# One written order for TensorE from the key tiles on, new places for its small steps, and eight block stores on ScalarE's queue

## The chip, the cores and the metric

The kernel runs on one core of one Trainium2 chip. Five engines work side by side, each through its own instructions in order: TensorE (PE in the profile, its weight loads PEld), VectorE (DVE), ScalarE (ACT), GpSimd (POOL) and SyncE (SP), which issues most transfers. The metric is device time in microseconds (us) of the whole program, the median of three runs.

## The reference

One layer of a hybrid decoder, for a sequence of 256 positions and a width of 2048, all in float32:

```
h    = rms_norm(x, attn_norm_g)
proj = h @ w_in                          # 2048 -> 4448 columns
r, k, v, w, a, g = split(token_shift(proj[: shifted part]))
c_q, c_kv, k_pe  = split(proj[rest])
y_rwkv = rwkv7_mixer(r, k, v, w, a, g)   # 16 heads of 64: a recurrence over positions,
                                         # then group norm, a bonus term and a gate
y_mla  = mla_mixer(c_q, c_kv, k_pe)      # 8 heads: up-projections, rotary keys, causal softmax
x = x + concat(y_rwkv, y_mla) @ w_out
h = rms_norm(x, ffn_norm_g)
x = x + (silu(causal_conv3(h @ w_gate)) * (h @ w_up)) @ w_down     # 5632 wide
out = rms_norm(x, final_norm_g)
```

The recurrence per head and position is state = state * w + (state a) b + v k, y = state r. The kernel computes it in four chunks of 64 positions: inside a chunk as products of matrices (Gram matrices, a triangular solve), and from chunk to chunk through the state.

## The kernel before, in words

**Big products.** Every weight comes from memory in pieces of 128 x 1024 float32 (`piece`, line 125). ScalarE casts a piece to a rounded part `hi` (line 133), VectorE makes the rest `lo` (line 134), and TensorE multiplies hi by both parts of the activations and lo by the high part. Three buffers each hold raw pieces, `hi` and `lo`. A tile of the input projection is 128 columns for all 256 positions: two pieces of 24 matmuls each, `in_tile` (line 194) or, written as a generator, `part_c` (line 789). `yield`s divide it into steps of eight matmuls, three steps a piece, six a tile. Tile 0 is the two low-rank inputs, 1 to 8 the keys, 9 to 16 the r's, 17 to 24 the values, 25 and 26 gate and rotary key, 27 to 34 the latents of attention.

**Small products between them.** Each key tile is normalized, shifted (`shifted`), multiplied into its block, squared, and its squares summed by `key_ss` (line 475). `decay` (line 411) forms four pairs of head groups' decays from the low-rank tile: eight records of `lw` and eight of `la` on TensorE (line 420), one on rows 0 to 63 and the other on rows 64 to 127, and a chain on ScalarE and VectorE. `key_norms` and `key_norms_p` turn the sums of squares into norms (`pmt`, line 500). After an r tile come its `bonus` sums (line 526), and after every second one `gram` (line 529): for a pair of head groups the products of two chunks at a time, on two row halves `h` (line 542), masked by VectorE into `G1` (line 547), and three transposes of the block (line 562). After the second and the fourth pair the corner blocks of G1 go to memory, 16 stores each, on SP's queue (line 555). `solve_load` reads them back, and `solve` (line 586) is a chain of 62 VectorE operations with two round trips to memory behind it, which leave the inverse in `TT` and `T11`. `values` transposes the value tiles (line 632).

**The recurrence.** `corner_r`, `corner_t` (R, T) complete the inverses with 32 x 32 products (lines 648, 661). Then for each chunk and each half of the heads: `rows` and `rows_state` (w, x), `solved` (i), `update` of the state (u), `out_state` and `out_local` (s, o), each 16 records of 64-wide products (line 686) with copies on VectorE or ScalarE between dependent ones.

**PSUM.** Eight banks: three `mm` for big products, three `ch` and two `at` for the rest. The bonus sums hold a `ch` bank through all r tiles. The key sums hold an `at` bank until the norms are formed.

**What sets the order.** The tile framework places every instruction of an engine by a simulated timeline, except where an order is fixed by hand. Up to the value tiles it places TensorE's work itself; the small steps are put on a list (`pend`) and issued behind the next tile. From the latents on, TensorE's order is fixed (`manual_schedule`, line 1137): `STREAM` is the list of big products, cut into steps, and `PLAN` the list of small steps; a number in PLAN is how many steps of the stream go before the next small step. Other engines' orders stay with the framework. The letters are in `small` (line 1120): for instance `w00`, `R0`, `S1` (scores of head 1), `P` (transposed weights of attention), `A` (attention's product), `N`, `G`, `Y` (group norm, gate and transposes), `X` (transposes of the sum x). In STREAM `l` is a latent tile, `q`, `Q`, `K`, `v` up-projections, `W` the output projection, `F` the first half of the feed-forward part.

## Time and profile before

| | before |
|---|---|
| median of three runs | 1170.52 us (1168.86 to 1172.1) |
| profiled execution: time | 1171.28 us |
| profiled execution: span | 1169.3 us, granted TensorE clock 0.995 on average |
| TensorE busy | 1151.5 us, 98% |
| VectorE busy | 807.0 us, 69% |
| ScalarE busy | 610.0 us, 52% |
| read from memory | 210.85 MB, 183 GB/s over the span |

The span runs from the first to the last instruction. Matmuls are pipelined and their ends are modelled, so "busy" is not "at full rate": in a timeline the distance from one start to the next says more. A matmul of 64-wide or larger float32 operands leaves two records. The granted clock is the share of full speed that the chip allowed TensorE in a stretch.

### The profile page before, as it was taken

To read this page: it belongs to the slowest core of one execution; us is meant where nothing else is said; L and a number is where in the kernel's file an instruction comes from. 1 tells how busy PE (TensorE), PEld (TensorE's weight loads), DVE (VectorE), ACT (ScalarE), POOL (GpSimd) and SP (SyncE) were. 2 spreads that over 40 slices of the span, in tenths; PEclk is the share of its full clock that TensorE was granted. 3 is DMA by queue.
4 is the path that set the end of the run, shared out by engine and by line. 5 is a ranking of instruction groups with operands and counts; after the bars stand their busy time and mean duration, and the time that the engine had idled before them with its cause. 6 is when DMAs were issued, how large, how long until landed. Compare 5 with 4: busy or idle time off the path is not lost.

```text
span 1169.3 us, 19472 instructions
## 1 busy us (share of the span) xinstructions
PE 1151.5 (98%) x7669; PEld 1018.2 (87%) x7669; DVE 807.0 (69%) x1333; ACT 610.0 (52%) x912; POOL 18.5 (2%) x45
## 2 busy tenths in 40 slices
PE   9999999999999999999999999999999999999996
PEld 9899999999878888888888888888888888888885
DVE  6897669746997577777767774544677777775653
ACT  6884346445653465555555553333455555554441
POOL 1200000000000000000000000000000000000000
PEclk9999999999999999999999999999999999999999
DMA  9645456715635555555555655665555565576672
GB/s 329 198 142 166 136 166 199 216 46 163 194 126 178 193 175 175 197 184 196 194 191 192 197 189 190 197 190 192 195 198 190 189 198 185 194 234 199 209 216 79
DMA packets 71227, 216.24 MB, mean 185 GB/s; under 512 B 17648, under 2 KB 18032, under 8 KB 71136
## 3 DMA queue, kind: packets, MB, share of 16 engines
q1 hardware_dynamic: 70208, 212.89, 56.2%
q10 hardware_dynamic: 576, 1.39, 0.4%
q8 instruction: 60, 0.98, 0.4%
q0 software_dynamic: 352, 0.72, 0.3%
q14 instruction: 31, 0.25, 0.1%
HBM read 210.85 MB, written 3.41 MB: 183 GB/s over the span
## 4 chain that ended last, share of the span: by engine, by line
PE 88%; DMA 4%; DVE 3%; ACT 2%; issue 1%; SPq 1%; ACTq 0%; DVEq 0%
PE mm L1080 27%; PE mm L1091 14%; PE mm L808 8%; PE mm L189 7%; PE mm L187 7%; PE mm L188 7%; PE mm L164 5%; PE mm L793 3%; PE mm L167 3%; PE mm L867 2%; DVE lo L134 1%; PE px L686 1%; PE pg L542 1%; DMA raw<-in_win 1%; PE py L686 1%
## 5 line engine op out<-in xcount | busy, mean ns | idle before, releaser
L134 DVE TENSOR_TENSOR lo<-raw,hi 128x1024 fp32r<-128x1024 f32 x376 | 459.8, 1223 | 269.2 <-ACT hi L133 198.9
L133 ACT CAST hi<-raw 128x1024 fp32r<-128x1024 f32 x376 | 395.7, 1053 | 422.5 <-PE mm L1080 126.1
L1080 PE MATMUL mm<-z,hi 128*128 128x512 f32 x1408 | 351.7, 392 | 0.8 <-DVE z L1032 0.8
L1080 PEld LDWEIGHTS mm<-z,hi 128*128 128x128 f32 x1408 | 251.5, 188 | 44.3 <-DVE z L1032 1.2
L1091 PEld LDWEIGHTS mm<-z,lo 128*128 128x128 f32 x1408 | 186.4, 188 | 14.9
L1091 PE MATMUL mm<-z,lo 128*128 128x256 f32 x1408 | 189.1, 276 | 0.0
L189 PE MATMUL mm<-hi,hl 128*128 128x512 f32 x336 | 130.7, 389 | 0.0
L188 PE MATMUL mm<-lo,hh 128*128 128x512 f32 x336 | 130.7, 389 | 0.0
L187 PE MATMUL mm<-hi,hh 128*128 128x512 f32 x336 | 119.7, 389 | 0.0
L164 PE MATMUL mm<-x,hi 128*128 128x256 f32 x768 | 103.0, 282 | 0.2 <-ACT hi L133 0.2
L164 PEld LDWEIGHTS mm<-x,hi 128*128 128x128 f32 x768 | 93.8, 188 | 2.0 <-ACT hi L133 0.4
L189 PEld LDWEIGHTS mm<-hi,hl 128*128 128x128 f32 x336 | 63.1, 188 | 13.2
L188 PEld LDWEIGHTS mm<-lo,hh 128*128 128x128 f32 x336 | 63.1, 188 | 13.1
L187 PEld LDWEIGHTS mm<-hi,hh 128*128 128x128 f32 x336 | 63.0, 188 | 12.9
L167 PE MATMUL mm<-x,lo 128*128 128x256 f32 x384 | 55.3, 281 | 0.0
L808 PE MATMUL mm<-hi,yhi 128*128 128x512 f32 x128 | 50.7, 396 | 0.0
L808 PE MATMUL mm<-lo,yhi 128*128 128x512 f32 x128 | 50.5, 395 | 0.0
L808 PE MATMUL mm<-hi,ylo 128*128 128x512 f32 x128 | 50.3, 393 | 0.0
L167 PEld LDWEIGHTS mm<-x,lo 128*128 128x128 f32 x384 | 48.8, 188 | 1.1 <-issue 1.0
L793 PE MATMUL mm<-x,hi 128*128 128x256 f32 x256 | 34.6, 286 | 0.0
L793 PEld LDWEIGHTS mm<-x,hi 128*128 128x128 f32 x256 | 31.6, 192 | 0.7
L808 PEld LDWEIGHTS mm<-hi,ylo 128*128 128x128 f32 x128 | 24.1, 188 | 5.3 <-DVE ylo L965 0.4
(294 smaller groups left out, 1120.6 us busy)
## 6 DMA issues: line engine op xcount, KB each, us to landing
raw<-in_wgu SPq DMA_DIRECT2D x176, 512.0 KB, 3.3
raw<-in_wdn SPq DMA_DIRECT2D x88, 512.0 KB, 4.2
raw<-in_win SPq DMA_DIRECT2D x70, 512.0 KB, 3.9
raw<-in_wout SPq DMA_DIRECT2D x32, 512.0 KB, 3.3
raw<-in_wuq SPq DMA_DIRECT2D x6, 512.0 KB, 4.4
xraw<-in_xT SPq DMA_DIRECT2D x4, 512.0 KB, 6.1
xt<-in_x SPq DMA_DIRECT2D x4, 512.0 KB, 7.5
raw<-in_wuv SPq DMA_DIRECT2D x4, 512.0 KB, 4.8
```

Of the source, the lines that this page charges most:

```text
L133: S.copy(hi, raw)
L134: last_lo[0] = V.tensor_tensor(lo, raw, hi.bitcast(F32), ALU.subtract).ins
L164: PE.matmul(acc[:, :T], hi[:, j * P:(j + 1) * P], act(kt0 + j)[:, s, :], start=first and j == 0 and s == 0, stop=False)
L167: i = PE.matmul(acc[:, :T], lo[:, j * P:(j + 1) * P], act(kt0 + j)[:, 0, :], start=False, stop=last and j == n - 1)
L187: PE.matmul(accs[tb], ah, wh, start=first and j == 0, stop=False)
L188: PE.matmul(accs[tb], ah, wl, start=False, stop=False)
L189: i = PE.matmul(accs[tb], al, wh, start=False, stop=last and j == n - 1)
L686: PE.matmul(dst[HS[h], a_ * 64:(a_ + 1) * 64], lhsT, rhs, start=begin and a_ == 0, stop=True, skip_group_check=True)
L793: PE.matmul(acc[:, :T], w[:, j * P:(j + 1) * P], act(j)[:, s, :], start=first and m == 0, stop=last and m == len(ops) - 1)
L808: PE.matmul(accs[tb], act, w, start=first and j == 0 and act is ah and w is wh, stop=last and j == 1 and act is al)
L1080: PE.matmul(accs[i], pcs[p][0][:, j * P:(j + 1) * P], z_hl(h * 8 + j), start=i not in seen, stop=False, skip_group_check=True)
L1091: PE.matmul(accs[i][:, :T], lo[:, j * P:(j + 1) * P], z_hl(h * 8 + j)[:, 0, :], start=False, stop=last and j == 7, skip_group_check=True)
```

## The change

TensorE's order is now fixed from the fourth key tile on, by the same STREAM and PLAN, and both lists are new. `pend` and `flush` are gone; key, r and value tiles become steps of the stream (`t4` to `t24`), and what was on the list becomes small steps with letters of their own. Two pieces of work are done in another way: the second half of a Gram product takes its two banks from `at` instead of `ch`, and of the last 16 corner stores the eight of the second row half are issued by ScalarE's queue.

```
+    def front_tile(i):
+        acc = mm()
+        for h in range(2):
+            yield from part_c(acc, piece(a["win"][i, h]), lambda k: x_hl(h * 8 + k), 8, h == 0, h == 1)
+            if h == 0:
+                yield
+        if i < 9:
+            key_done(i - 1, acc)
+        elif i < 17:
+            r_done(i - 9, acc)
+        else:
+            vt[i - 17] = shifted(acc, i)
+        yield
...
     def decay(pp):
-        with tc.high_priority(), tc.manual_schedule(engines={mybir.EngineType.PE}):
-            for g in range(2):
+        for g in range(2):
...
-        def gram(p=p, pp=pp):
+    def gram(pp, w):
...
-            for w in range(2):
-                pg = [ch("pg") for _ in range(2)]
+        pg = [(at if w else ch)("pg") for _ in range(2)]
...
-                            nc.sync.dma_start(dLv[b, c, :, h, hf * 4:hf * 4 + 4, :],
+                        (nc.scalar if h and hf else nc.sync).dma_start(
+                            dLv[b, c, :, h, hf * 4:hf * 4 + 4, :],
...
+    def turn_b(pp):
...
+        for cs in ((0, 1), (2,)):
+            pt = ch("pt")
...
     def solve():
+        for c in range(4):
+            nc.gpsimd.memset(UV[c][64:128], 0.0)
...
     small = {
-        "o": out_local, "r": latent_root, "b": spread, "c": swap, ...
+        "o": out_local, "r": latent_root, "f": spread, "c": swap, ...
+        "n": norm2, "D": decay, "E": key_done, "k": key_ss, "t": turn_b, "m": key_norms, "p": key_norms_p, "b": bonus,
+        "a": gram, "B": bonus_rows, "L": solve_load, "Z": solve, "V": values,
     }
     STREAM = """
-    l00 l01 l02 l03 l10 l11 l12 l13 q1 q0 v0 K0 Q0 K1 Q1 v1 K2 Q2 K3 Q3 W100 W110 W120 W130 W001 W021
-    W011 W031 F
+    t4 t5 t6 t7 t8 t9 t10 t11 t12 t14 t13 t15 t16 t18 t17 t20 t19 t21 t23 t22 t24 l00 l01 l02 l03 l10
+    l11 l12 l13 q0 q1 v0 K0 Q0 Q1 K2 K1 Q2 v1 K3 Q3 W100 W110 W120 W130 W001 W021 W011 W031 F
     PLAN = """
-    12 w00 18 r0 4 R0 R1 T0 w01 1 i00 i01 w11 u00 u01 w10 o01 T1 x11 x10 o00 s10 i10 i11 s11 u10 w20 u11
-    w21 o10 o11 1 x20 x21 1 s21 2 i20 w30 i21 1 s20 u20 u21 w31 1 o21 1 o20 x31 x30 s31 1 g 1 i31 i30 1
-    s30 1 o30 6 r1 o31 7 b1 c 4 e 7 S0 S1 5 S3 S2 1 P0 1 N0 4 P1 h0 2 P3 h1 A0 1 A1 1 S4 1 P2 1 S5 A2 1 A3 3
-    S6 2 P4 3 P5 A4 A5 S7 2 P6 1 P7 A6 A7 9 N1 1 G10 5 G00 2 G01 5 Y01 11 Y10 1 Y00 4 G11 2 Y11 26 X00
-    11 X10 X21 4 X01 4 X11 2 X20 2 X30 X31 9 n
+    2 D0 1 E0 E1 2 D1 E2 4 k1 k0 2 D2 5 k2 1 D3 5 k4 1 k3 7 k5 7 t0 1 k6 6 t1 k7 1 m 1 p a00 1 t2 a01 b1
+    7 b0 3 b2 2 t3 b3 2 a10 a11 5 b5 4 a20 a21 5 b4 3 b6 2 a30 2 b7 B a31 4 L 1 Z 19 V0 10 V1 2 w00 12
+    V2 12 V3 14 R1 2 R0 1 w01 1 T0 1 i00 i01 w11 u00 u01 w10 o01 x11 o00 x10 i11 s10 i10 s11 w20 u10 w21
+    u11 o10 1 x21 T1 x20 r0 1 o11 1 s21 s20 i20 i21 3 g o21 w30 3 u20 w31 h1 u21 o20 x30 x31 i30 s31 s30
+    i31 6 o30 3 r1 4 o31 2 f1 1 c 1 e 5 S1 3 h0 1 S0 8 S3 2 S2 2 P0 P1 N0 3 A1 S4 1 A0 P3 1 P2 2 S5 A3
+    A2 2 P4 S6 5 P5 S7 A4 P6 A5 2 A6 N1 P7 1 A7 3 G10 17 G00 2 G01 9 G11 1 Y10 2 Y11 1 Y01 2 Y00 32 X01
+    9 X21 3 X10 X00 3 X11 5 X31 2 X20 X30 5 n
```

`b` is the bonus sums now, and the old `b` is `f`. `h0` and `h1` split the gate's weights; `g` loads group norm's weights. The text below calls a place in the new order by the sum of the numbers ahead of it in PLAN: R1 stands at step 156, and the 21 tiles of the stream's first part fill steps 1 to 126.

## The prediction

> **What bounds the kernel now.** I read the page's first part, then TensorE's waits, then TensorE's timeline with its starts, since a start-to-start distance shows lost time that a busy share hides.

> ```profile
> PE 1151.5 (98%) x7669; PEld 1018.2 (87%) x7669; DVE 807.0 (69%) x1333; ACT 610.0 (52%) x912; POOL 18.5 (2%) x45
> ```

> TensorE is busy 98% of a span of 1169.3 us. The change removes no matmul, so it can only gain where TensorE's instructions stand further apart than they need to. Everything it moves lies between some 43 us (the fourth key tile) and 420 us (the second norm); behind that the two kernels issue the same work. TensorE's waits in the front part (37 to 205 us) are few:

> ```profile
> PE lw L420 <- ACT early L396: 0.8, 1, 0.8
> PE la L420 <- DVE hb L177: 0.4, 1, 0.4
> PE pv L632 <- DVE sh L386: 0.2, 1, 0.2
> PE ssP L475 <- ACT ksq L471: 0.2, 1, 0.2
> ...
> PE pT L661 <- ACT RT L652: 0.4, 1, 0.4
> PE pT L661 <- DMA TT<-dT: 0.3, 1, 0.3
> ```

> The last two are of the recurrence. These six sum to 2.3 us: shown waits alone would not repay a new order. The rest sits in instructions that are busy but slow, and the timeline finds it.

> **Part 1, the gram products: -5.1 us.** The columns are start, time, instruction, and how many records.

> ```profile
> 98.14 1.98 PE L164 MATMUL mm<-x,hi 128*128 128x256 f32 x16
> 99.95 1.08 PE L167 MATMUL mm<-x,lo 128*128 128x256 f32 x8
> ...
> 101.30 1.16 PE L542 MATMUL pg<-AR,BK 64*128 64x128 f32 x16
> 102.39 2.15 PE L164 MATMUL mm<-x,hi 128*128 128x256 f32 x16
> ...
> 105.65 1.16 PE L542 MATMUL pg<-AR,BK 64*128 64x128 f32 x8
> 106.73 0.38 PE L164 MATMUL mm<-x,hi 128*128 128x256 f32 x1
> 107.05 1.16 PE L542 MATMUL pg<-AR,BK 64*128 64x128 f32 x8
> 108.13 1.74 PE L164 MATMUL mm<-x,hi 128*128 128x256 f32 x13
> ...
> 155.29 1.16 PE L542 MATMUL pg<-AR,BK 64*128 64x128 f32 x8
> ```

> Sixteen records on the two halves of the rows, issued in turns, take 102.39 - 101.30 = 1.09 us. The other half-gram of the same pair is split by the free buffers: eight records of one row half, one big matmul, eight of the other. It runs from 105.65 to 108.13; less 0.12 us for the big matmul between, that is 2.36 us for the same work. Before, both halves of a gram draw on the three `ch` buffers, of which the bonus sums hold one; the change takes the second half's two tiles from the two `at` buffers and issues the halves in turns. So the second half should also take 1.09 us: 1.27 us saved, four times (this first one; the last is the split one that ends the list) = 5.1 us. At nothing in return: the two `at` buffers are free once the key sums have been read, and the first gram stands behind the key norms in the new order.

> **Part 2, the decay products: -0.9 us.**

> ```profile
> 46.35 0.48 PE L420 MATMUL lw<-early,lora 64*128 64x256 f32 x1 [0.80 <-ACT early L396]
> ...
> 47.42 0.74 PE L167 MATMUL mm<-x,lo 128*128 128x256 f32 x4
> ...
> 50.78 0.70 PE L420 MATMUL la<-early,lora 64*128 64x256 f32 x2 [0.36 <-DVE hb L177]
> 51.41 0.38 PE L167 MATMUL mm<-x,lo 128*128 128x256 f32 x1
> 51.72 0.48 PE L420 MATMUL lw<-early,lora 64*128 64x256 f32 x1
> ...
> 52.78 0.62 PE L167 MATMUL mm<-x,lo 128*128 128x256 f32 x3
> ```

> The first decay is whole, 1.07 us. The second is torn: 50.78 to 52.78 less one big matmul is 1.9 us, so 0.8 us too long. Of the other two one is torn as well, by a shorter piece; 0.6 us is my estimate from the second's 0.8. The new order issues each whole: -1.4. Against that D0 now stands two steps into the fourth key tile. A step is eight matmuls: 1.81 us for sixteen (98.14 to 99.95) make 0.91 us. It comes some 0.45 us earlier than before while its tanh comes no earlier: +0.5.

> **Part 3, key sums and value turns: -0.4, and +1.0 new.** The two waits of 0.2 us in the list go: the value turn that waited now stands 14 steps behind its last tile. But two places look tight. k4 stands at step 22: from D0's end at 47.4, twenty steps of 0.91 and some five us for three decays and three key sums make 71, and before, TensorE waited for k4's squares until about 71.6: +0.4. The key norms' transpose (p) stands two steps, 1.8 us, behind the last key sum; before,

> ```profile
> 89.57 0.50 PE L475 MATMUL ssP<-cst,ksq 128*128 128x2 f32 x4
> ...
> 93.02 0.34 DVE L496 RECIPROCAL mtok<-mt 128x32 f32<-128x32 f32 x1
> ```

> VectorE had the norms at 93.36, 3.8 us after that sum began, with other work between. From the start of k7 to p there are now 2.2 us (0.36 for k7's own and the two steps): a wait of 0 to 1.6, and I take 0.6. Behind p on TensorE stand all later products, so such a wait counts in full.

> **Part 4, the recurrence's corners: -3.7 us.** Three windows of the busy table: length, TensorE, its weight loads, VectorE, ScalarE, GpSimd, then granted clock, DMA share, GB/s; and the instructions there.

> ```profile
> 228.35:231.76 3.41, 2.72 (x158) 2.50 (x152) 2.13 (x8) 1.15 (x2) 0.00 (x0) 1.00 1.06 237
> 231.76:238.58 6.82, 6.82 (x112) 6.30 (x108) 1.51 (x3) 2.68 (x5) 0.00 (x0) 0.50 0.40 153
> 238.58:249.00 10.42, 10.36 (x342) 9.84 (x339) 4.96 (x11) 4.59 (x13) 0.00 (x0) 1.00 0.01 3
> ...
> 227.83 2.42 PE L648 MATMUL pR<-T,G 32*32 32x32 f32 x128
> ...
> 231.19 1.54 PE L661 MATMUL pT<-TT,RT 32*32 32x32 f32 x62 [0.32 <-DMA TT<-dT]
> ```

> After 2.42 us of 32-wide products and two waits the granted clock is 0.50 for 6.82 us. At most half of that, 3.4 us, is lost; I take 3.0, since small products are partly bound by their issue. The third row says that a long run of 64-wide products keeps the full clock. The new order parts R1, R0, w01 and T0 by one or two steps of big products, so a stretch with only 32-wide work, at most 1.2 us, no longer comes up. With the two waits (0.7) that makes -3.7. [...]

> The runs of the recurrence are as many as before (13 each by the plan strings), so joining steps saves nothing by count. But the new run u20 w31 u21 o20 x30 x31 i30 s31 s30 i31 has ten dependent steps.

> ```profile
> 249.83 1.15 PE L686 MATMUL px<-ST,AR 64*64 64x64 f32 x32
> 250.91 1.22 PE L793 MATMUL mm<-x,hi 128*128 128x256 f32 x8
> ```

> Two steps take 1.08 us. x30 follows u20 by three steps, 1.6 us, in which two VectorE operations must end; i30 follows x30 by one step, 0.54 us, in which one copy must. The unit for a VectorE operation that is queued ahead is the split, 1.23 us (below). So 0 to 2.4 us; I take 0.7.

> **Part 5, the solve and the ScalarE queue: +0.6 us.**

> ```profile
> 153.05 7.60 SPq L555 DMA_DIRECT2D dL<-G  x16
> ...
> 167.88 1.23 DVE L593 TENSOR_TENSOR Lp<-Lp,Mp 128x1024 f32<-128x1024 f32 x1 [3.05 <-DMA Lp<-dL]
> ...
> 217.38 1.15 DVE L603 COPY tp<-Tq 128x1024 f32<-128x1024 f32 x1
> ...
> ACT hi L133 <- PE mm L164: 41.7, 20, 4.3
> ```

> Sixteen stores keep SP's queue 7.6 us, 0.47 each. Eight move to ScalarE's, so the load of dL can go out up to 3.8 us sooner. On ScalarE the eight wait for VectorE's masks and hold up the weight casts behind them, at most 3.8 us and the masks; but ScalarE there stands waiting for TensorE to free a `hi` buffer (41.7 us in 20 waits), two pieces ahead, and a piece is three steps, 2.7 us. So 0; without that cover up to 3.8. Before, 227.83 less the last gram's end (155.29 + 1.09) = 71.4 us lay between gram and R, of which the solve on VectorE took 217.38 - 167.88 = 49.5. With half of the 3.8 saved, R can run 69.5 us after the gram. In the new order R1 stands 74 steps behind a31 (82 to 156): 67.3 us, with four value turns and w00 between, some 2.6: 69.9. Level. In a fixed order any delay of the solve stops TensorE; 0 to 3, I take 0.6.

> **Part 6, attention: +1.2 us.**

> ```profile
> L857 ACT COPY qr<-mm x4: 366/370/373, 275.0 to 280.9; 128x256 f32<-128x256 f32 x4
> ...
> 289.00 1.22 DVE L881 TENSOR_TENSOR qr<-qr,cosR 128x1024 f32<-128x1024 f32 x1 [0.80 <-DMA qs<-qr]
> ...
> 295.35 1.22 DVE L883 TENSOR_TENSOR qr<-qr,qs 128x1024 f32<-128x1024 f32 x1
> ...
> 295.97 0.34 PE L929 MATMUL psc<-cmb,idb 128*128 128x384 bf16 x1
> ```

> The rotated queries were ready at 296.57, just in time for the first scores. Now S1 stands 12 steps behind the q tiles where S0 stood 16: 3.6 us sooner, and directly behind Q0 itself. The rotation has slack only inside VectorE: from 289.00 to 296.57 its three operations need 3.7 of 7.6 us. So a wait of 0 to 3.6; I take 1.2. For the other new joins from S3 to A7 I add 0.5.

> **Sum.** Gains 5.1 + 1.4 + 0.4 + 3.7 = 10.6; new costs 0.5 + 1.0 + 0.7 + 0.6 + 1.2 + 0.5 = 4.5; net -6.1 us. The profiled execution took 1171.28 us (span 1169.3 and 2.0 around it), 0.8 over the median of 1170.52 us. So 1165.2 beside the profiled one, 1164.4 us as a median.

> **Rivals.**
> A, 13%: the granted clock falls again, in one of the long joined runs or for a cause that the order does not touch. For it: it fell with 2.72 of 3.41 us busy. Against it: the third window. 3.0 us come back: 1167.4.
> B, 6%: the second half-grams still run in two parts, since an `at` buffer is not free. Against it: nothing but the key sums uses `at` there. 5.1 us come back: 1169.5.
> C, 12%: the fixed front order waits for VectorE, which is full from 60 to 90 us:

> ```profile
> 60.00:90.00 30.00, 29.76 (x247) 28.84 (x246) 30.00 (x67) 24.96 (x44) 1.85 (x2) 1.00 0.46 144
> ```

> TensorE then cannot run ahead by what parts 2 and 3 save, and the waits at p, R1 and S1 double: 4 us more, 1168.4.
> D, 7%, slower: the solve comes late and TensorE stands at R1. Before, a scheduler could put other products there; now none may pass. From a solve of about 50 us on, each microsecond is one lost; it must stretch to some 60 us, by VectorE working off tiles with priority, before all is eaten and 3.5 us more. Then 1175. Against it: as many tiles stand beside the solve as before.
> The forecast keeps 62%.

> **Numbers.** About 0.3%, 3.5 us, can be told from no change: under 1167.0 is faster, over 1174.0 slower. Faster: the forecast nearly whole (0.60), half of A, a third of C, 0.01 of B: 0.72. Slower: D, 0.07. The same: 0.21. Low end: no new wait at all, 10.6 - 0.5 saved, 1160.4, and a little for attention's old waits, 1159.5. High end: B's 1169.5, which takes in A and C. Left out are D and a tail of A with C.

> **What would show it.** Right: all L542 rows in 16s of 1.09 us; no granted clock below 1.00 between 200 and 300 us; R1 at about 218 us (227.8 less 5.4 for the front and 3.6 for the four stream steps by which it moved up); waits at pmt, psc and pT near 1 us each or less; the first feed-forward matmul some 6 us earlier. Wrong: eights of L542; a window at 0.50; a TensorE wait of several us for TT or T11, or at pmt.

## The result and the profile after

The changed kernel takes 1161.94 us (median of six runs, 1160.44 to 1164.16) beside 1170.28 us for the kernel before, six runs on the same chip: a ratio of 0.9933 [0.9922 to 0.9945] (here and below with its 95% interval), some 8 us less. Four of the six executions have a mean granted clock of 0.997 or 0.998 and took 1160.4 to 1162.1 us; the other two, at 0.996, took 1164.0 and 1164.2 us. The prediction was 1164.4 us, in a range of 1159.5 to 1169.5. The profiled execution after took 1161.08 us, span 1158.9. The profiled pair thus differs by 10.2 us, more than the medians, because the one execution lies above its median and the other below.

The page's first part after, then TensorE's waits (total us, times, longest):

```profile
PE 1139.1 (98%) x7669; PEld 1008.6 (87%) x7669; DVE 809.0 (70%) x1333; ACT 611.8 (53%) x912; POOL 18.6 (2%) x45
...
PE pmt L480 <- DVE mtok L476: 1.6, 1, 1.6
...
PE la L407 <- ACT tw L412: 1.0, 1, 1.0
PE psc L912 <- DVE kn L166: 0.9, 1, 0.9
PE mm L1058 <- DVE z L1010: 0.8, 1, 0.8
PE lw L407 <- ACT early L384: 0.8, 1, 0.8
PE py L650 <- DVE ST L694: 0.4, 1, 0.4
PE mm L845 <- DVE kn L166: 0.4, 1, 0.4
...
PE pT L625 <- ACT RT L616: 0.2, 1, 0.2
```

As many TensorE instructions as before, 12.4 us less busy time, and no less waiting (TensorE is idle for 19.8 us of the span, 17.8 before): what the new order saved was slowness inside busy stretches, and it paid part of it back in waits of about 1 us.

Where the time went shows in the starts of TensorE's first matmul of a stage. The first rows are before (fourth key tile, first latent, first product of the output projection, first of the feed-forward part), the next ones after:

```profile
43.13 0.39 PE L164 MATMUL mm<-x,hi 128*128 128x256 f32 x2
195.14 0.36 PE L793 MATMUL mm<-x,hi 128*128 128x256 f32 x1
328.88 0.40 PE L808 MATMUL mm<-hi,yhi 128*128 128x512 f32 x1
434.55 0.48 PE L1080 MATMUL mm<-z,hi 128*128 128x512 f32 x1
```

```profile
43.65 0.39 PE L757 MATMUL mm<-x,hi 128*128 128x256 f32 x2
189.12 0.28 PE L757 MATMUL mm<-x,hi 128*128 128x256 f32 x1
319.23 0.40 PE L772 MATMUL mm<-hi,yhi 128*128 128x512 f32 x1
423.74 0.40 PE L1058 MATMUL mm<-z,hi 128*128 128x512 f32 x1
```

| stretch | before, us | after, us | difference | the prediction's terms there |
|---|---|---|---|---|
| up to the fourth key tile | 43.1 | 43.7 | +0.5 | 0 |
| fourth key tile to latents | 152.0 | 145.5 | -6.5 | parts 1 to 3: -5.4 |
| latents to output projection | 133.7 | 130.1 | -3.6 | parts 4 and 5, S1: -1.2 |
| output projection to feed-forward | 105.7 | 104.5 | -1.2 | other joins: +0.5 |
| rest | 734.8 | 735.2 | +0.4 | 0 |

Some small steps cross a mark. w00 (some 0.7 us) stands before the latents after and behind them before; one and a half of the four value turns (again some 0.7 us) crossed the other way, so the second and third rows can be compared as they stand. One of the eight transpose steps of the sum x (0.4 us) crossed the fourth mark, so like for like the fourth row is -0.8.

The marks of the prediction, in TensorE's timeline after: a whole gram, 32 records in one run, and the corner of the recurrence.

```profile
118.53 1.07 PE L757 MATMUL mm<-x,hi 128*128 128x256 f32 x8
119.53 2.06 PE L518 MATMUL pg<-AR,BK 64*128 64x128 f32 x32
121.52 1.19 PE L757 MATMUL mm<-x,hi 128*128 128x256 f32 x8
...
217.33 1.20 PE L612 MATMUL pR<-T,G 32*32 32x32 f32 x64
218.46 2.11 PE L757 MATMUL mm<-x,hi 128*128 128x256 f32 x16
220.50 1.20 PE L612 MATMUL pR<-T,G 32*32 32x32 f32 x64
...
225.01 1.20 PE L625 MATMUL pT<-TT,RT 32*32 32x32 f32 x64 [0.21 <-ACT RT L616]
```

Both halves of the gram now take 121.52 - 119.53 = 1.99 us; before, the first took 1.09 and the split second 2.36. R1 starts at 217.33, without a wait, where the prediction had about 218. Two marks came out higher than it said: the wait at pmt is 1.6 us, not near 1 or less, and the first feed-forward matmul is 10.8 us earlier, not some 6. In this execution the granted clock stays whole across the corner (columns as in the prediction; the clock is the third figure from the right):

```profile
216.90:220.30 3.40, 3.40 (x85) 3.23 (x83) 0.68 (x1) 0.00 (x0) 0.00 (x0) 1.00 1.15 254
220.30:223.70 3.40, 3.40 (x92) 2.88 (x90) 1.52 (x2) 2.03 (x3) 0.00 (x0) 1.00 0.66 254
223.70:227.10 3.40, 3.19 (x80) 2.96 (x80) 2.29 (x3) 1.68 (x4) 0.00 (x0) 1.00 0.56 135
```

### The profile page after: what moved, and what is told of

Read it like the earlier page. It is cut to its first block, busy times and chain, and to the rows that moved or that the text cites. A ratio compares the mean times of both kernels' runs of the same rounds, so it can differ in the third digit from the quotient of the medians.

```text
span 1158.9 us, 19465 instructions
## 1 busy us (share of the span) xinstructions
PE 1139.1 (98%) x7669; PEld 1008.6 (87%) x7669; DVE 809.0 (70%) x1333; ACT 611.8 (53%) x912; POOL 18.6 (2%) x45
## 3 DMA queue, kind: packets, MB, share of 16 engines
HBM read 210.85 MB, written 3.41 MB: 185 GB/s over the span
## 4 chain that ended last, share of the span: by engine, by line
PE 87%; DVE 6%; DMA 3%; ACT 2%; issue 1%; SPq 0%; POOL 0%; ACTq 0%; DVEq 0%
PE mm L1058 28%; PE mm L1069 14%; PE mm L757 10%; PE mm L772 8%; PE mm L176 7%; PE mm L178 7%; PE mm L177 7%; DVE lo L134 2%; DMA raw<-in_win 2%; PE mm L845 2%; ACT hi L133 1%; PE px L650 1%; PE py L650 1%; PE pg L518 1%; DMA xraw<-in_xT 1%
## 5 line engine op out<-in xcount | busy, mean ns | idle before, releaser
L133 ACT CAST hi<-raw 128x1024 fp32r<-128x1024 f32 x376 | 395.6, 1053 | 417.3 <-PE mm L1058 130.3
L177 PE MATMUL mm<-lo,hh 128*128 128x512 f32 x336 | 130.7, 389 | 0.0
L757 PE MATMUL mm<-x,hi 128*128 128x256 f32 x928 | 119.9, 279 | 0.0
L757 PEld LDWEIGHTS mm<-x,hi 128*128 128x128 f32 x928 | 111.4, 188 | 0.8
L177 PEld LDWEIGHTS mm<-lo,hh 128*128 128x128 f32 x336 | 63.1, 188 | 13.0
L757 PE MATMUL mm<-x,lo 128*128 128x256 f32 x464 | 64.4, 281 | 0.0
L757 PEld LDWEIGHTS mm<-x,lo 128*128 128x128 f32 x464 | 57.4, 188 | 1.9 <-issue 1.2
L772 PEld LDWEIGHTS mm<-hi,yhi 128*128 128x128 f32 x128 | 24.1, 188 | 4.8
L772 PEld LDWEIGHTS mm<-lo,yhi 128*128 128x128 f32 x128 | 24.1, 188 | 4.8
```

The lines of the kernel that those rows point to most:

```text
L133: S.copy(hi, raw)
L177: PE.matmul(accs[tb], ah, wl, start=False, stop=False)
L757: PE.matmul(acc[:, :T], w[:, j * P:(j + 1) * P], act(j)[:, s, :], start=first and m == 0, stop=last and m == len(ops) - 1)
L772: PE.matmul(accs[tb], act, w, start=first and j == 0 and act is ah and w is wh, stop=last and j == 1 and act is al)
```

## The experiments

The theory: the second bank of the grams is worth some 5 us, the parted corner some 3.7, the rest of the new order a little or a cost. The rivals: the new order as a whole makes the gain, or the fallen clock has another cause. Each time is compared with runs of the kernel before on the same chip.

**1. The grams' bank taken back (from after).**

```
-        pg = [(at if w else ch)("pg") for _ in range(2)]
+        pg = [ch("pg") for _ in range(2)]
```

> The kernel after, with both halves of a Gram product on the ch banks again. Theory (the banks are worth some 5 us, whoever sets the order): TensorE now waits for VectorE's masks at a01, a11 and a21, some 1.2 to 1.9 us each; 1166 to 1168 us. Rival (the fixed order in itself pairs the row halves, banks are free in time): records still in 16s without waits, 1162 us, as the kernel after.

Measured: 1167.67 us, 0.9981 [0.9969 to 0.9992]; 5.7 us over after. Its timeline at the first gram:

```profile
102.46 0.46 PE L518 MATMUL pg<-AR,BK 64*128 64x128 f32 x2 [0.18 <-DVE G L523]
103.35 1.16 PE L518 MATMUL pg<-AR,BK 64*128 64x128 f32 x14 [0.43 <-ACT BKt L545]
```

The second half is in pieces of 2 and 14 records, still on both row halves, and TensorE waits 3.1 us in five places for VectorE to empty a gram bank. At the next gram the granted clock falls behind such a wait:

```profile
122.65 0.46 PE L518 MATMUL pg<-AR,BK 64*128 64x128 f32 x2 [1.26 <-DVE G L523]
...
121.89:125.29 3.40, 2.10 (x21) 1.85 (x22) 2.28 (x7) 0.00 (x0) 0.46 (x1) 1.00 0.65 183
125.29:128.69 3.40, 3.40 (x19) 3.40 (x18) 1.32 (x4) 1.04 (x1) 1.44 (x2) 0.50 0.18 25
```

The theory holds: without the bank, between a quarter and a third of the gain is left. But the 5.7 us are of another make than what the kernel before loses here. There the halves are issued in eights without a wait; here it is waits and, in this execution, 3.4 us at half clock.

**2. The bank alone (from before).**

```
-                pg = [ch("pg") for _ in range(2)]
+                pg = [(at if w else ch)("pg") for _ in range(2)]
```

> The kernel before, with nothing changed but the banks of the second half-grams (at instead of ch). Theory (the banks alone make the 5 us; the framework's own order pairs the row halves once both banks are free): all records in 16s, 1165 us. Rival (the framework's order still splits them, the written order is needed): 1170 us, eights of L542 as before.

Measured: 1165.09 us, 0.9963 [0.995 to 0.9976]: 5.25 us less. The framework's own order issues both halves whole once they have banks; the written order isn't needed for that.

```profile
99.98 2.06 PE L542 MATMUL pg<-AR,BK 64*128 64x128 f32 x32
...
165.67 0.44 PE L632 MATMUL pv<-cst,sh 128*128 128x128 f32 x2 [2.63 <-DVE sh L386]
```

The second row is new: TensorE arrives sooner at the turn of the first value tiles and waits 2.63 us for VectorE there (0.2 before). And the granted clock falls to 0.50, there and at the corner:

```profile
163.60:167.00 3.40, 1.33 (x12) 1.34 (x13) 3.37 (x9) 2.97 (x5) 0.00 (x0) 0.99 0.24 75
167.00:170.40 3.40, 3.40 (x19) 3.40 (x18) 3.26 (x9) 1.30 (x4) 0.00 (x0) 0.50 0.69 241
225.00:228.40 3.40, 3.03 (x161) 2.88 (x154) 2.27 (x6) 1.16 (x2) 0.00 (x0) 1.00 1.01 267
228.40:231.80 3.40, 3.40 (x38) 3.08 (x36) 0.37 (x2) 1.99 (x3) 0.00 (x0) 0.50 0.57 225
```

**3. The corner parted, alone (from before).**

```
-    12 w00 18 r0 4 R0 R1 T0 w01 1 i00
+    12 w00 18 r0 4 R0 1 R1 1 w01 1 T0 1 i00
...
-    1 o30 6 r1
+    1 o30 3 r1
```

> The kernel before, with R0, R1, w01 and T0 one step apart each, the steps taken back ahead of r1. Theory (32-wide products in one piece let the clock fall): full clock around 230 us, waits for RT and TT gone; 3.7 us less for clock and waits, 0.6 more for three further runs: 1167 us; or 1168 us if the executions of before without the fall (1168.8 and 1169.0 at a mean clock of 0.998, against 1170.5 at 0.994) tell the clock's price better than the window does. Rival (the fall has another cause): 1170 us with a window at 0.50.

Measured: 1169.09 us, 0.9991 [0.9983 to 1.0]: 1.25 us less. In all 11 runs the mean clock is 0.997 or 0.998; in 21 of the 24 runs of the kernel before beside it, it was 0.994 to 0.996. The fall is gone, as expected (a wait of 0.3 us for RT stays):

```profile
228.80:232.20 3.40, 3.40 (x108) 3.19 (x101) 1.78 (x5) 0.58 (x1) 0.00 (x0) 1.00 1.00 279
232.20:235.60 3.40, 3.14 (x87) 2.75 (x87) 1.29 (x2) 2.00 (x3) 0.00 (x0) 1.00 0.57 230
```

It is worth less than expected. In the two profiled executions the first latents start together, at 195.14 and 195.12 us; by the first up-projection of the keys the parted corner has brought 286.15 - 283.61 = 2.5 us (the first row is before):

```profile
286.15 1.07 PE L867 MATMUL mm<-cl,hi 128*128 128x256 f32 x8
```

```profile
283.61 1.07 PE L867 MATMUL mm<-cl,hi 128*128 128x256 f32 x8
```

And the medians show half of that; the interval goes from nothing to 2.0 us. The profiled execution of before is a usual one: its mean clock of 0.995 is also the median of the 24 runs. The 56 runs of the kernel before that stand beside the ten experiments give a price of their own: 1171.0 us on average at a mean clock of 0.994 (17 runs) and 1169.0 at 0.998 (six runs), a difference of 2 us.

**4. The corner joined again (from after).**

```
-    V2 12 V3 14 R1 2 R0 1 w01 1 T0 1 i00
+    V2 12 V3 18 R0 R1 T0 w01 1 i00
```

> The kernel after, with R0 R1 T0 w01 in one run at step 160, as they stood before. Theory (32-wide products in one piece with a wait let the granted clock fall): a window at 0.50 for some 6.8 us right behind T0, and 3 us more, 1165 us. Rival (the fall before had another cause): full clock throughout, and only a wait for RT of under 1 us: 1162 to 1163 us.

Measured: 1164.95 us, 0.9951 [0.9935 to 0.9968]; 3.0 over after. The clock falls again, for 10.2 us where it was 6.8 before, but a wait has come in as well:

```profile
226.23 1.92 PE L625 MATMUL pT<-TT,RT 32*32 32x32 f32 x64 [3.48 <-ACT RT L616]
...
223.20:233.40 10.20, 7.17 (x126) 6.65 (x128) 4.14 (x7) 3.91 (x7) 0.00 (x0) 0.50 0.29 93
```

T0 directly behind R0 and R1 waits for copies of R. So the 3.0 us are the clock and this wait together; the run doesn't price the clock.

**5. R0 and R1 side by side, the rest parted (from after).**

```
-    V2 12 V3 14 R1 2 R0 1 w01 1 T0 1 i00
+    V2 12 V3 16 R1 R0 1 w01 1 T0 1 i00
```

> The kernel after with R1 and R0 in one run (2.3 us of 32-wide products in a row, no wait behind them), w01 and T0 still one step apart each. [...] Rival (the fall needs TensorE to stand still as well, as in the 0.7 us of waits of the kernel before): full clock, 1161.9 us less one run's 0.2.

Measured: 1164.77 us, 0.9962 [0.995 to 0.9974]. This run was to separate 32-wide work from waiting, and it doesn't:

```profile
219.23 2.21 PE L612 MATMUL pR<-T,G 32*32 32x32 f32 x128
...
225.10 1.12 PE L650 MATMUL px<-UV,G 128*64 128x64 f32 x16 [1.82 <-ACT RT L616]
```

The two R's hold their banks longer, w01 waits 1.82 us for one, and the granted clock is 0.50 from 224.70 to 228.10 us; in the 3.40 us before that TensorE is only 1.53 us busy. Whether 2.2 us of 32-wide products alone would lower the clock stays open.

**6. All stores on SP's queue (from after).**

```
-                        (nc.scalar if h and hf else nc.sync).dma_start(
+                        nc.sync.dma_start(
```

> The kernel after, with all sixteen of the last stores on SP. Theory (the path from the last Gram product to R1 is level, under 1 us of slack): the load of dL goes out 2 to 3 us later, TensorE waits at pR for T11 or at pT for TT for 1 to 2 us; 1163 to 1164 us. Rival (the queue of the stores is off the path): 1162 us, no wait at R.

Measured: 1161.94 us, 0.9932 [0.9916 to 0.9949]: the time of after, which the interval can tell to some 2 us. The load of the stored blocks goes out at 154.09 us, after has it at 152.43, and R1 waits in neither.

```profile
152.43 0.34 SPq L558 DMA_DIRECT2D Lp<-dL  x1
```

```profile
154.09 0.34 SPq L558 DMA_DIRECT2D Lp<-dL  x1
```

But this profile has a wait that after hasn't: w00 stands 1.70 us for ScalarE's copies of the value tiles.

```profile
182.68 0.45 PE L650 MATMUL px<-UV,G 128*64 128x64 f32 x8 [1.70 <-ACT UV L603]
```

Behind the sixteen stores on SP's queue two of ScalarE's weight casts wait 2.39 and 3.88 us for their pieces from memory; that the late copies follow from this is argued, not shown. R1 then starts at 218.65 us, 1.3 us later than in after, so it says little that R1 doesn't wait. My theory, a wait of 1 to 2 us at R, isn't borne out, and in the medians the queue is worth nothing that can be told from noise.

In after the load thus went out 1.7 us sooner, less than the 3.8 us for which the last eight stores hold SP's queue in this run, and the medians show no gain.

**7. The key norms' turn three steps later (from after).**

```
-    1 m 1 p a00 1 t2 a01 b1
-    7 b0
+    1 m 1 a00 1 t2 a01 b1
+    2 p 5 b0
```

> The kernel after, with the transpose of the key norms (p) three steps later, a00, a01 and the rest as they are. Theory (TensorE stood 1.6 us for VectorE at p, nothing else waits there): the wait goes, 1160.3 us. Rival (another wait takes its place at a00 or a01, which need the at bank that the same VectorE operations free): 1161 to 1162 us.

Measured: 1160.12 us (four runs), 0.991 [0.9894 to 0.9926]: 1.8 less than after, about the 1.58 us of the wait. The two intervals still touch (0.9926 here, 0.9922 for after). All four runs have a mean clock of 0.997 or 0.998; against the four such runs of after, with a median of 1161.45 us, 1.3 us are left. The wait is gone and nothing near it has taken its place:

```profile
105.41 0.27 PE L480 MATMUL pmt<-cst,mtok 128*32 128x128 f32 x1
```

Much later, w01 waits 0.5 us for RT and an up-projection 0.8 us for `kn` instead of 0.4.

**8. More room in attention too (7, and S1 and two X steps later).**

```
-    e 5 S1 3 h0
+    e 6 S1 2 h0
...
-    3 X11 5 X31 2 X20 X30 5 n
+    3 X11 2 X20 3 X31 2 X30 5 n
```

> The kernel after with p three steps later, S1 one step later and X20 three steps ahead of X30. Theory (each of TensorE's waits at pmt 1.6, at psc 0.9 and at the first z 0.8 goes without another in its place): 1158.5 us. Rival (S1's wait for kn moves to the next product that reads the same bank, the z wait to the later parts): 1160 us, as with p alone.

Measured: 1159.77 us, 0.9918 [0.9905 to 0.9931], not told apart from 7. The scores' wait is gone, but the feed-forward's for `z` grew from 0.8 to 1.2 us, and the up-projection's for `kn` stays at the 0.8 of run 7. Both wait for VectorE, which the order doesn't make faster. 7 and 8 are the fastest versions tried.

**9. After's order up to the value tiles, before's behind (from after).** The old STREAM and PLAN from the latents on, and w00 where it fits. Two of the changed lines:

```
...
-    V2 12 V3 14 R1 2 R0 1 w01 1 T0 1 i00 i01 w11 u00 u01 w10 o01 x11 o00 x10 i11 s10 i10 s11 w20 u10 w21
+    b7 B a31 4 L 1 Z 19 V0 10 V1 14 V2 8 w00 4 V3 14 r0 4 R0 R1 T0 w01 1 i00 i01 w11 u00 u01 w10 o01 T1 x11
...
```

> The kernel after up to V3, and from w00 on the order of the kernel before (same places behind the front's 126 steps). Theory (front and rest add up: the front brings some 5 to 6 us, the recurrence with the clock 2 to 3, attention nothing): 1164 to 1166 us, with the granted clock at 0.50 behind R0 R1 T0 in most executions. Rival (nearly all of the gain is in the front, and the tail's new order is worth nothing): 1162 us.

Measured: 1165.61 us, 0.9971 [0.9962 to 0.998]; 3.7 over after. Its profile, of an execution 2 us over the run's median, has a wait of 3.6 us for RT at T0 (0.4 before) and, as before, 6.8 us at half clock. So behind a shorter front the old corner costs more than it did before; that this is most of what the new tail brings is argued from this one profile.

**10. Bank and parted corner (from before), the edits of 2 and 3 together.**

> The kernel before with the two things that the earlier runs name, and nothing else of the change: the second half-grams on the at banks, and R0, R1, w01, T0 one step apart. Theory (these two are most of the change and add up, 5.25 and 1.25 us): 1163.8 us, full clock in most executions; then the written front order and all the other moves are worth 2 us. Rival (the framework's order fills the room with new waits, as the 2.6 us at pv with the bank alone): 1165 us.

Measured: 1164.17 us, 0.9951 [0.9939 to 0.9964], about 5.7 us less by the ratio and 4.8 by the two medians (before ran at 1168.98 beside it). Two small edits thus bring most of the change. What the written order adds is what is left to 0.9933, some 2 us; the two intervals overlap a little, so its size is uncertain. In this profile the value turn waits 2.0 us, and 3.4 us at half clock follow; after has neither, since V0 stands 24 steps behind the last gram. The profiled execution is the slowest of the five, 1167.55 us at a mean clock of 0.995; the other four, at 0.997 or 0.998, took some 1164 us, so the fall can't be usual here.

## Why the prediction was right, point by point

**Part 1, right in cause and size.** 5.1 us predicted; 5.25 measured by putting the bank in. Counted in the timelines from each start to the next, the gram products take 13.0 us before and 8.4 after, 4.6 less. That taking the bank out costs nearly the same, 5.7, is chance: those are waits and a fallen clock (run 1).

**Part 2, right in sum.** Counted the same way, the products of the four decays take 5.5 us before and 4.3 after, and their waits 1.2 and 1.7: 0.7 us less, 0.9 predicted. (A decay is four records of `lw` and four of `la`, not eight of each as said further up.) One term had the wrong cause: I let D1 keep its wait of 0.4 for `hb`. It waits 0.97 for ScalarE's `tw`, to read the first decay out of its bank:

```profile
46.38 0.48 PE L407 MATMUL lw<-early,lora 64*128 64x256 f32 x1 [0.75 <-ACT early L384]
...
51.42 0.48 PE L407 MATMUL la<-early,lora 64*128 64x256 f32 x1 [0.97 <-ACT tw L412]
```

**Part 3, the place right, the price at its top.** The wait at p is 1.58 us; I had taken 0.6 of 0 to 1.6, and run 7 shows that it counts nearly in full (1.3 to 1.8 us). VectorE has the norms 3.8 us after the last key sum began, as it had before, and p stands only two steps behind that sum:

```profile
95.58 0.51 PE L463 MATMUL ssP<-cst,ksq 128*128 128x2 f32 x4
...
98.33 0.72 DVE L473 TENSOR_SCALAR mt<-ssP 64x16 f32<-64x16 f32 x4
99.08 0.35 DVE L476 RECIPROCAL mtok<-mt 128x32 f32<-128x32 f32 x1
...
99.58 0.27 PE L480 MATMUL pmt<-cst,mtok 128*32 128x128 f32 x1 [1.58 <-DVE mtok L476]
```

The wait at k4 (0.4) didn't come. Of rival C, the wait at p came; those at R1 and S1 didn't grow.

**Part 4, the mechanism right, the size wrong.** This is the term that was mis-sized: 3.0 for the clock and 0.7 for waits. Parting the corner does keep the clock (run 3), but it is worth 2.5 us in the profiled pair and 1.25 [0 to 2.0] in the medians, for 3.7 predicted. I took products at half the clock for nearly twice as slow. Eight big ones in the corner are (2.01 us from start to start before, 1.13 in run 3), but the 32 records of i00 took 1.90 us for 1.40: at half clock they lost 0.50 us, not half of their time, and the 0.4 that I took off the 3.4 for small products was too little. What bounds these besides the clock, no run isolates. Run 3 also pays for three more changes between small and big products than the kernel before, 0.6 us by what I expected, so some 3.1 were due there. Rival A didn't come in the profiled execution. But the two executions of after at a mean clock of 0.996 are 2 to 3 us longer than the others, so the clock may still fall in some; no trace here shows where. The long joined run waits 0.44 us, once, for 0.7 taken.

**Part 5, "level" held.** R1 waits for nothing, so the 0.6 was not spent. The room is small: in after the second of the loads that R1 needs (L586) goes out at 212.1 us and takes some 4.5 to land, by estimate 0.7 us ahead of R1. Run 6 shows no more room than that, since its R1 came later as well. In the medians ScalarE's queue cost nothing and brought nothing.

**Part 6, one wait found, the rest free.** S1 waits 0.89 us for 1.2 taken, by the trace for `kn`, VectorE's scaled copy of the key tile, and not for the rotated queries. But VectorE made that copy right behind the last operation of the rotation, so the crowding on VectorE that I expected is part of it:

```profile
282.70 1.22 DVE L861 TENSOR_TENSOR qr<-qr,qs 128x1024 f32<-128x1024 f32 x1
283.83 0.41 DVE L166 TENSOR_TENSOR kn<-mm,rrB 128x256 f32<-128x256 f32 x1
```

The 0.5 for other joins didn't come: that stretch lost 1.2 us, 0.8 like for like.

**The sum.** The net was -6.1; the medians say -8.3, and the profiled pair -10.2. In that pair all three stretches gained more than predicted, by 1.1, 2.4 and 1.7 us, although part 4 was too large: that the total is this close is partly luck.

In the front, waits rose by 1.7 us for 1.1 predicted, but work fell by 8.2 for 6.5. What I left out shows in the big products: the same ones take 122.1 us before, in 42 unbroken runs, and 119.2 after, in 28 runs. I had asked what joining small steps saves only for the recurrence, where it saves nothing by count. No run isolates this. From the latents to the output projection I charged 1.8 us of new waits, net; TensorE's waits there are 1.8 us before and 1.9 after, because the new ones took the place of old ones of attention, for which I had credited nothing.

The value turns can't explain the excess: their wait of 2.0 to 2.6 us (runs 10 and 2) stands neither in before nor in after. It is what a faster front meets in the old order, and so a reason, argued from two profiles and not shown, for the 2 us between run 10 and after. That the written order was needed for the pairing of the halves, as I had it in part 1 ("issues the halves in turns"), is refuted by run 2.

## What to carry to other kernels

Look for products on two row halves that run in eights where sixteens are possible, and ask which bank the second half lacks: one line brought nearly two thirds of this change. Count the unbroken runs of big products in the old and the new order, not the small steps alone. Price a lowered clock from the times of many executions at different mean clocks (2 us here), not from half the length of its fall (3.4 us). And when a front is made faster, price each small step behind it by the time at which its input is ready, not by the wait that the old order showed.

## What the runs showed of the hardware

```profile
97.80:99.58 1.78, 0.21 (x2) 0.04 (x2) 1.67 (x8) 0.96 (x4) 0.00 (x0) 1.00 0.78 228
```

The traces thus show falls behind stretches hardly busy and nearly full, and none behind this pause. What sets them apart, no run isolates.
